# A list scheduler that is told of the tensor engine's divisions

## The chip, the cores and the metric

The kernel runs on one core of a Trainium2 chip. The metric is device microseconds of one execution; lower is better. Three runs of the kernel before took 1682.05, 1683.13 and 1686.35 us, median 1683.13 us.

The core has a tensor engine (PE; its weight loads are shown as an engine of their own, PEld), a vector engine (DVE), a scalar engine (ACT), GpSimd (POOL) and a queue that issues DMAs (SP). Each of them takes its instructions strictly in the order in which they were written; semaphores hold an instruction back until what it needs is there.

## The reference

One layer of a hybrid encoder trunk on 512 tokens of width 1024, in float32:

```
h = rmsnorm(x, norm_mix)
y_a = rwkv7_mixer(h @ wi[:, :OFF_HGRN], ...)        # 16 heads of 64
y_b = hgrn2_mixer(h @ wi[:, OFF_HGRN:OFF_SSM], ...) # 8 heads of 128
y_c = mamba2_mixer(h @ wi[:, OFF_SSM:OFF_GATE], ...) # 4 groups of 8 heads of 64
gates = sigmoid(h @ wi[:, OFF_GATE:]).reshape(b, s, 3, D_MODEL)
merged = gates[:, :, 0] * (y_a @ wb[:1024]) + gates[:, :, 1] * (y_b @ wb[1024:2048])
       + gates[:, :, 2] * (y_c @ wb[2048:])
x = x + merged @ w_out
gate, up = split(rmsnorm(x, norm_ffn) @ w_ffn_in, 2)
x = x + (silu(gate) * up) @ w_ffn_out
out = rmsnorm(x, norm_final)
```

The RWKV mixer is a recurrence over tokens that is computed in chunks of 64; HGRN2 needs decayed scores within chunks, built from small blocks; Mamba-2 is computed in chunks of 128.

## The kernel before, in words

The three mixers share the tensor engine. Dense projections split every float32 operand in a high and a low part (tiles `hh` and `hl`, `wh` and `wl`) and run three passes of 128 x 512 for each pair of 128 x 128 weights (`mm3`, `dense_h`, `dense_cm`). Those, the transposes against `ident` and most other matmuls use all 128 rows and 128 columns of the array. Three kinds of work use a part of it:

- the RWKV chain (`quads`, called from `r_stage1` and `r_chain`): 64 rows by 64 columns, one quarter of the array for each of two heads;
- the HGRN score blocks (`blocks` in `hgrn`): 128 rows by 32 columns, four strips side by side; 16 matmuls make a group, with a PSUM tile `m` (so named in the profile, as `m<-X` or `m<-q,k`);
- a few with 128 rows by 64 columns (the first HGRN level, a narrow projection), 64 rows by 128 columns (two transposes in `r_inverse`) and 32 rows.

I call such a pair of row and column counts a division of the array.

Nothing is written in the order of the source. The class `Recorder` takes down every operation with what it depends on, and `flush` then writes the instructions of all engines by list scheduling: it runs a clock of its own for each engine with estimated durations (`cost`, `passes`, `xfer`), takes the engine that is free first, and gives it, of the operations that are ready by then, the one of the lowest priority number. RWKV's chain has 0, its first stage 1, HGRN 2, Mamba-2 3, the 24 gate projections 4 (PSUM tile `g`, weights `gwh` and `gwl`), the first three parts of the merge 5, and the rest 6. So gates serve as filler wherever nothing more urgent is ready, and everything from the last part of the merge on comes after the mixers. ACT has an exception already: work with the table that is loaded may go ahead of work that needs another table.

For the tensor engine `flush` keeps, for each of the 4 x 4 cells of 32 rows by 32 columns, when its weights were loaded and when its last pass ends (`self.pe`); `passes` tells it how long an operation loads weights, how long each pass streams, and which cells it uses. It lets a load run under the pass before it, whatever the divisions of the two.

Of the kernel before, what the change touches and what calls it, by code (L numbers as in the profile page):

```python
# [74 lines left out]
class Queue:  # L75


    def __init__(self, rec, name):
        self.rec, self.name = rec, name
# [5 lines left out]
class Recorder:  # L85
# [6 lines left out]
    def __init__(self, tc):  # L92
        self.tc, self.nc = tc, tc.nc
        for e in self.ENGINES:
            if e != "gate":
                setattr(self, e, Queue(self, e))
        self.ops, self.done = [], 0
        self.prio = 0
        self.writes, self.reads, self.acc = {}, {}, {}
        self.gate, self.tiles_dram = {}, set()  # L100
        self.tiles, self.proto, self.views = [], {}, set()
        self.tags, self.prev, self.before, self.dead = {}, {}, {}, set()
        self.free = dict.fromkeys(self.ENGINES, 0.0)
        self.table = None
        self.dma = 0.0

        self.pe, self.pe_last = [[(0.0, 0.0)] * 4 for _ in range(4)], 0.0
        self.parts = {}
        self.port = {"vector": 0.0, "gpsimd": 0.0}

# [91 lines left out]
    def passes(self, out, method, args):  # L202


        n = 1
        for d in out.shape[1:]:
            n *= d
        load = args[1].shape[-1] / 1200
        if method == "transpose" or args[1].dtype == F32R:
            ps = [n / (1200 if method == "transpose" else 2226)]  # L210
        else:
            ps = [n / 1200] * 2
        rows, cols = ((q[1] // 32, -(-q[2] // 32)) for q in (self.region(args[1]), self.region(out)))
        return load, ps, [(i, j) for i in range(*rows) for j in range(*cols)]

    def shares(self, eng, method, args, kw, out):

# [84 lines left out]
    def flush(self):  # L302
        ops, lo, n = self.ops, self.done, len(self.ops)
        succ = [[] for _ in range(n - lo)]
        need = [0] * (n - lo)
        ready = [0.0] * (n - lo)
        fut = {e: [] for e in self.ENGINES}
        now = {e: [] for e in self.ENGINES}

        def lat(j, eng):  # L310
            e = ops[j][0]
            if e == eng:
                return {"vector": 0.13, "sync": 2.0, "tensor": -0.3}.get(e, 0.0)
            if e == "sync":
                return 1.0 if ops[j][9] > 0.5 else 2.05
            if e == "gate":
                return 0.0
            if eng == "tensor":
                return 0.17 if e == "scalar" else 0.15
            return 0.21 if e == "tensor" else 0.14  # L320

        def push(k):
            heapq.heappush(fut[ops[lo + k][0]], (ready[k], k))

        for k in range(n - lo):
            op = ops[lo + k]
            for j in op[5]:
                if j >= lo:
                    succ[j - lo].append(k)
                    need[k] += 1  # L330
                else:
                    ready[k] = max(ready[k], ops[j][8] + lat(j, op[0]))
            if not need[k]:
                push(k)
        order, left = [], n - lo
        while left > len(order):
            best = None
            for e in self.ENGINES:
                if now[e]:
                    t = self.free[e]  # L340
                elif fut[e]:
                    t = max(self.free[e], fut[e][0][0])
                else:
                    continue
                if best is None or t < best[0]:
                    best = (t, e)
            t, e = best
            while fut[e] and fut[e][0][0] <= t:
                k = heapq.heappop(fut[e])[1]
                heapq.heappush(now[e], (ops[lo + k][6], k))  # L350
            k = now[e][0][1]
            if e == "scalar" and self.switch(ops[lo + k]) and ops[lo + k][6] and t - ready[k] < 3:
                c = [x for x in now[e] if not self.switch(ops[lo + x[1]])]
                if c:
                    k = min(c)[1]
            now[e].remove((ops[lo + k][6], k))
            heapq.heapify(now[e])
            op = ops[lo + k]
            if e == "scalar" and self.switch(op):
                t += 1.28  # L360
                self.table = op[7]
                order.append(-1 - lo - k)
                left += 1
            if e == "tensor":
                load, ps, parts = op[9]
                loaded = max([ready[k]] + [self.pe[i][j][0] for i, j in parts])
                end = max(self.pe[i][j][1] for i, j in parts)
                for d in ps:
                    loaded = self.pe_last = max(loaded + load, end + 0.003, self.pe_last + 0.006)
                    end = loaded + d  # L370
                for i, j in parts:
                    self.pe[i][j] = (loaded, end)
                op[4] = end - t
            t = max(t, ready[k])
            if e in ("vector", "scalar"):

                if self.parts.get(e) not in (None, op[11]) and t - self.free[e] < 0.1:
                    t = max(t, self.free[e] + 0.11)
                self.parts[e] = op[11]
            if e != "gate" and op[10]:  # L380
                t = max(t, self.port["gpsimd" if e == "vector" else "vector"])
                self.port[e] = t + op[4]
            op[8] = t = t + op[4]
            if e != "gate":
                self.free[e] = op[8]
                order.append(lo + k)
                if e == "sync":
                    op[8] = self.dma = max(op[8] + 0.65, self.dma) + op[9]
            else:
                left -= 1  # L390
            for m in succ[k]:
                ready[m] = max(ready[m], op[8] + lat(lo + k, ops[lo + m][0]))
                need[m] -= 1
                if not need[m]:
                    push(m)
        with self.tc.manual_schedule():
            for j in order:
                if j < 0:
                    self.nc.scalar.preload_act_table_set(ops[-1 - j][7])  # L399
                    continue  # L400
                eng, method, args, kw = ops[j][:4]
                getattr(getattr(self.nc, eng), method)(*[self.resolve(x) for x in args],  # L402
                                                       **{k: self.resolve(x) for k, x in kw.items()})
                ops[j][2:4] = (None, None)
        self.done = n
# [1232 lines left out]
```

## Time and profile before

| | before |
|---|---|
| median of 3 runs | 1683.13 us |
| the profiled execution | 1686.82 us, its span 1685.0 us |
| PE busy | 1630.3 us (97%) |
| PEld busy | 1321.4 us (78%) |
| DVE busy | 1031.7 us (61%) |
| ACT busy | 835.6 us (50%) |
| POOL busy | 267.1 us (16%) |
| granted PE clock, mean | 0.993 |

The span runs from the first instruction to the last; the execution's own time has 1.8 us around it. All recorded operations have one source line in the profile (L402, the line where `flush` issues them; L411 in the changed kernel), so work is told apart by its tiles. In a row such as `PE L402 MATMUL rw<-Ot,SB 64*64 64x64 f32` the part `64*64` is the division, rows by columns. A plain float32 matmul stands in the trace as two passes with a weight load each, a transpose or a pass over split operands as one.

### The profile page before, as it was taken

To read this page: it belongs to the slowest core of one execution; us is meant where nothing else is said; L and a number is where in the kernel's file an instruction comes from. 1 tells how busy PE (TensorE), PEld (TensorE's weight loads), DVE (VectorE), ACT (ScalarE), POOL (GpSimd) and SP (SyncE) were. 2 spreads that over 40 slices of the span, in tenths; PEclk is the share of its full clock that TensorE was granted. 3 is DMA by queue.
4 is the path that set the end of the run, shared out by engine and by line. 5 is a ranking of instruction groups with operands and counts; after the bars stand their busy time and mean duration, and the time that the engine had idled before them with its cause. 6 is when DMAs were issued, how large, how long until landed. Compare 5 with 4: busy or idle time off the path is not lost.

```text
span 1685.0 us, 32049 instructions
## 1 busy us (share of the span) xinstructions
PE 1630.3 (97%) x12302; PEld 1321.4 (78%) x12302; DVE 1031.7 (61%) x2327; ACT 835.6 (50%) x1523; POOL 267.1 (16%) x285
## 2 busy tenths in 40 slices
PE   6999999999999999999999999999999999999998
PEld 5787788777777787788898787777788888888886
DVE  5788888878687878757648748344453533333233
ACT  6666654555466547556647855333433533333222
POOL 1123221313122222003014204011020000000000
PEclk9999999999999999999999999999999999999999
DMA  5334323233233333334424545777572333333232
GB/s 160 85 85 101 90 61 97 77 95 92 65 90 93 86 80 97 90 91 116 122 76 138 154 135 162 241 232 226 175 219 76 113 94 94 94 94 94 95 99 76
DMA packets 291321, 192.09 MB, mean 114 GB/s; under 512 B 59053, under 2 KB 255047, under 8 KB 291167
## 3 DMA queue, kind: packets, MB, share of 16 engines
q1 hardware_dynamic: 291167, 190.04, 39.7%
q8 instruction: 97, 1.59, 0.4%
q14 instruction: 57, 0.47, 0.1%
HBM read 164.22 MB, written 25.76 MB: 113 GB/s over the span
## 4 chain that ended last, share of the span: by engine, by line
PE 81%; DMA 6%; ACT 4%; DVE 4%; issue 2%; SPq 1%; POOL 1%; POOLq 0%; ACTq 0%; DVEq 0%
PE d L402 23%; PE rd L402 17%; PE g L402 10%; PE rw L402 8%; PE rs L402 8%; PE m L402 8%; PE ru L402 7%; SPq L402 1%; ACT L399 1%; DMA wr<-in_w_in_dram 1%; DMA em<-ydram 1%; DMA a<-in_rwkv_a_up_dram 1%; DMA ab<-ydram 1%; DMA cb<-dcum 1%; DVE wl L402 1%
## 5 line engine op out<-in xcount | busy, mean ns | idle before, releaser
L402 DVE TENSOR_TENSOR wl<-wr,wh 128x512 fp32r<-128x512 f32 x267 | 188.4, 707 | 247.4 <-ACT wh L402 239.3
L402 ACT CAST wh<-wr 128x512 fp32r<-128x512 f32 x267 | 164.8, 619 | 342.2 <-PE d L402 119.9
L402 ACT CAST rgh<-rgr 128x512 fp32r<-128x512 f32 x142 | 87.9, 619 | 189.6 <-PE rd L402 89.6
L402 DVE TENSOR_TENSOR rgl<-rgr,rgh 128x512 fp32r<-128x512 f32 x142 | 100.7, 710 | 118.0 <-ACT rgh L402 116.3
L402 PE MATMUL d<-hh,wh 128*128 128x512 f32 (+1 forms) x368 | 147.8, 402 | 7.4 <-DVE q L402 3.5
L402 PE MATMUL d<-hh,wl 128*128 128x512 f32 (+1 forms) x368 | 144.7, 393 | 1.1 <-DVE wl L402 1.1
L402 PE MATMUL d<-hl,wh 128*128 128x512 f32 (+1 forms) x368 | 145.1, 394 | 0.0
L399 ACT ACT_TABLE_LOAD x105 | 134.7, 1283 | 1.8
L402 PE MATMUL rd<-hh,rgh 128*128 128x512 f32 (+1 forms) x324 | 129.6, 400 | 1.0 <-DVE k L402 0.5
L402 PE MATMUL rd<-hl,rgh 128*128 128x512 f32 (+1 forms) x324 | 128.9, 398 | 0.0
L402 PE MATMUL rd<-hh,rgl 128*128 128x512 f32 (+1 forms) x324 | 128.2, 396 | 0.0
L402 PEld LDWEIGHTS d<-hh,wh 128*128 128x128 f32 x368 | 69.5, 189 | 24.9 <-issue 4.4
L402 PE MATMUL g<-hh,gwh 128*128 128x512 f32 x192 | 80.3, 418 | 6.7 <-ACT gwh L402 4.2
L402 PEld LDWEIGHTS d<-hh,wl 128*128 128x128 f32 x368 | 69.4, 189 | 15.2 <-DVE wl L402 1.4
L402 POOL TENSOR_TENSOR X<-X,q 128x256 f32<-128x256 f32 x56 | 51.6, 930 | 181.7 <-ACT X L402 143.9
L402 PEld LDWEIGHTS d<-hl,wh 128*128 128x128 f32 x368 | 69.6, 189 | 12.7 <-issue 0.6
L402 PE MATMUL g<-hh,gwl 128*128 128x512 f32 x192 | 78.1, 407 | 0.2
L402 PE MATMUL g<-hl,gwh 128*128 128x512 f32 x192 | 77.9, 406 | 0.0
L402 PE MATMUL d<-wh,hh 128*128 128x256 f32 x256 | 73.5, 287 | 1.3 <-ACT v L402 0.8
L402 PEld LDWEIGHTS rd<-hh,rgh 128*128 128x128 f32 x324 | 61.3, 189 | 16.7 <-DVE k L402 1.6
L402 PE MATMUL d<-wl,hh 128*128 128x256 f32 x256 | 73.3, 286 | 0.0
L402 PE MATMUL d<-wh,hl 128*128 128x256 f32 x256 | 72.7, 284 | 0.0
(1509 smaller groups left out, 4294.4 us busy)
## 6 DMA issues: line engine op xcount, KB each, us to landing
wr<-in_w_in_dram SPq DMA_DIRECT2D x108, 256.0 KB
rgr<-in_w_in_dram SPq DMA_DIRECT2D x88, 256.0 KB
wr<-in_w_branch_dram SPq DMA_DIRECT2D x59, 256.0 KB
wr<-in_w_ffn_in_dram SPq DMA_DIRECT2D x58, 256.0 KB
gwr<-in_w_in_dram SPq DMA_DIRECT2D x96, 128.0 KB
rgr<-in_w_ffn_in_dram SPq DMA_DIRECT2D x30, 256.0 KB
wr<-in_w_ffn_out_dram SPq DMA_DIRECT2D x30, 256.0 KB
gdram<-gwr SPq DMA_DIRECT2D x24, 256.0 KB
```

The costliest lines, as they stand in the source:

```text
L399: self.nc.scalar.preload_act_table_set(ops[-1 - j][7])
L402: getattr(getattr(self.nc, eng), method)(*[self.resolve(x) for x in args], **{k: self.resolve(x) for k, x in kw.items()})
```

## The change

`passes` returns the division of an operation besides its cells. `flush` remembers the division of the last tensor operation (`pe_mode`) and does two things with it. If the division changes, the first weight load of the new operation may end no earlier than 0.09 us after the last pass on any of the 16 cells; that is, the estimate has the array drain. And while the division is a partial one, ready work of that same division goes before all other ready work, whatever its priority; within it the lowest number still goes first. When the whole array is in use, the choice is as before.

```
-        self.pe, self.pe_last = [[(0.0, 0.0)] * 4 for _ in range(4)], 0.0
+        self.pe, self.pe_last, self.pe_mode = [[(0.0, 0.0)] * 4 for _ in range(4)], 0.0, None
...
-        return load, ps, [(i, j) for i in range(*rows) for j in range(*cols)]
+        return load, ps, [(i, j) for i in range(*rows) for j in range(*cols)], (rows[1] - rows[0], cols[1] - cols[0])
...
+            if e == "tensor" and self.pe_mode not in (None, (4, 4)):
+                c = [x for x in now[e] if ops[lo + x[1]][9][3] == self.pe_mode]
+                if c:
+                    k = min(c)[1]
...
-                load, ps, parts = op[9]
+                load, ps, parts, mode = op[9]
                 loaded = max([ready[k]] + [self.pe[i][j][0] for i, j in parts])
                 end = max(self.pe[i][j][1] for i, j in parts)
+                if mode != self.pe_mode:
+
+                    loaded = max(loaded, max(x[1] for r in self.pe for x in r) + 0.09 - load)
+                    self.pe_mode = mode
```

All engines' orders shift with it, since the estimates decide what is ready when. The tensor engine issues the same 9526 operations (12302 passes); the first 88 and the last 2183 stand in the same order, and half of all are moved by 31 places or more. ACT gets three more table loads.

The first place is on PE near 295 to 302 us of the trace before. `m_1264`, `m_1266`, `m_1268` and `m_1269` are groups of HGRN blocks, `rw_508` and `rw_624` quarters of the RWKV chain, `rs` transposes and `d_1281` a projection of HGRN. Before:

```order
L402 MATMUL m_1264_3957<-X_1263_3786 32x32 x5
L402 MATMUL m_1266_4067<-X_1265_3881 32x32 x10
L402 MATMUL rd_562_4080<-xa_57_383,lwh_559_3931 128x512
...
L402 MATMUL rs_490_4095<-ident_1_93,v_462_3792 128x128 x4
L402 MATMUL m_1266_4067<-X_1265_3881 32x32 x6
L402 MATMUL d_1281_3784<-hl_3_176,wh_1283_3674 128x512
...
L402 MATMUL m_1269_4121<-q_1227_3137,k_1217_2598 32x32 x4
L402 MATMUL rw_624_4127<-UV_489_4108,KAo_480_4057 64x64 x16
L402 MATMUL rs_492_4151<-ident_1_93,BK_474_3569 128x128 x4
L402 MATMUL m_1269_4121<-q_1227_3137,k_1217_2598 32x32 x12
L402 MATMUL d_1281_3784<-hl_3_176,wh_1283_3674 128x512
```

The same operations now:

```order
L411 MATMUL rs_491_4049<-ident_1_93,AR_473_3497 128x128 x4
L411 MATMUL m_1264_4059<-X_1263_3853 32x32 x16
L411 MATMUL m_1266_4079<-X_1265_3870 32x32 x16
L411 MATMUL rw_624_4099<-UV_489_4032,KAo_480_4003 64x64 x16
L411 MATMUL rs_492_4118<-ident_1_93,BK_474_3547 128x128 x4
L411 MATMUL m_1269_4124<-q_1227_3145,k_1217_2686 32x32 x16
L411 MATMUL d_1281_4147<-hh_2_168,wh_1283_3659 128x512
```

A group of 16 blocks that stood in two pieces with other divisions between them now stands in one piece, and two groups follow each other.

The second place is on PE near 700 us, between two projections, `d_1598` and `d_1606`, that use the one PSUM tile `d` in turn; `g_2313` and `g_2299` are gates. Before:

```order
L402 MATMUL d_1598_9489<-hh_2_168,wl_1604_9107 128x512
L402 MATMUL m_1674_9686<-ident_1_93,k_1588_9484 128x128 x3
L402 MATMUL g_2313_8869<-hl_3_176,gwh_2324_9291 128x512
L402 MATMUL g_2313_8869<-hh_2_168,gwl_2325_9305 128x512
L402 MATMUL d_1606_9714<-hh_2_168,wh_1608_9176 128x512
```

Now, with 26 passes of 128 x 512 and 14 transposes between the two, of which the first and the last few are shown:

```order
L411 MATMUL d_1598_9356<-hh_2_168,wl_1604_9053 128x512
L411 MATMUL g_2299_9594<-hh_2_168,gwh_2301_8850 128x512
L411 MATMUL g_2299_9594<-hl_3_176,gwh_2301_8850 128x512
L411 MATMUL m_1674_9598<-ident_1_93,k_1588_9324 128x128
L411 MATMUL m_1586_9602<-ident_1_93,X_1585_9545 128x128 x4
...
L411 MATMUL g_2299_9594<-hh_2_168,gwl_2308_9626 128x512
L411 MATMUL g_2299_9594<-hh_2_168,gwh_2310_9649 128x512
L411 MATMUL g_2299_9594<-hl_3_176,gwh_2310_9649 128x512
L411 MATMUL g_2299_9594<-hh_2_168,gwl_2311_9653 128x512
L411 MATMUL g_2299_9594<-hh_2_168,gwh_2310_9649 128x512
L411 MATMUL d_1606_9684<-hh_2_168,wh_1608_9099 128x512
```

Gate `g_2299` was used up earlier before, and `g_2313` stood here; now there is more of the gates left at this place.

The third place is on PE near 640 us: `m_1526` reads `cb_1525`, which ACT copies out of the transposes `m_1524`. Before:

```order
L402 MATMUL rd_1896_8481<-hl_3_176,rgh_1901_7865 128x512
L402 MATMUL rd_1896_8481<-hh_2_168,rgl_1902_7886 128x512
L402 MATMUL g_2299_7544<-hh_2_168,gwl_2311_8004 128x512
L402 MATMUL m_1524_8850<-ident_1_93,X_1523_8760 128x128 x3
L402 MATMUL m_1526_8862<-v_1480_8081,cb_1525_8858 128x128 x2
L402 MATMUL m_1526_8862<-v_1481_8474,cb_1525_8858 128x128
```

Now:

```order
L411 MATMUL m_1524_8832<-ident_1_93,X_1523_8727 128x128 x3
L411 MATMUL d_1543_8837<-hh_2_168,wh_1545_8457 128x512
L411 MATMUL d_1543_8837<-hl_3_176,wh_1545_8457 128x512
L411 MATMUL d_1543_8837<-hh_2_168,wl_1546_8464 128x512
L411 MATMUL d_1543_8837<-hh_2_168,wh_1545_8457 128x512
L411 MATMUL d_1543_8837<-hl_3_176,wh_1545_8457 128x512
L411 MATMUL d_1543_8837<-hh_2_168,wl_1546_8464 128x512
L411 MATMUL m_1526_8855<-v_1480_7977,cb_1525_8846 128x128 x2
L411 MATMUL m_1526_8855<-v_1481_8357,cb_1525_8846 128x128
```

Six passes of a projection now stand between the transposes and what reads their copy.

## Rows read from the trace of the kernel before

**Rows 1.** The page: span, engines, granted clock, chain that ended last, table loads.
```profile
span 1685.0 us, 32049 instructions
PE 1630.3 (97%) x12302; PEld 1321.4 (78%) x12302; DVE 1031.7 (61%) x2327; ACT 835.6 (50%) x1523; POOL 267.1 (16%) x285
...
PE 81%; DMA 6%; ACT 4%; DVE 4%; issue 2%; SPq 1%; POOL 1%; POOLq 0%; ACTq 0%; DVEq 0%
...
L399 ACT ACT_TABLE_LOAD x105 | 134.7, 1283 | 1.8
```
**Rows 2.** Stretch and length; busy PE, PEld, DVE, ACT, POOL; PEclk, DMA, GB/s.
```profile
100.00:700.00 600.00, 581.16 (x7026) 462.97 (x7025) 485.89 (x1346) 336.37 (x635) 146.22 (x151) 0.99 0.34 86
700.00:1200.00 500.00, 485.87 (x2601) 399.26 (x2600) 287.56 (x517) 271.56 (x483) 88.73 (x90) 0.99 0.52 154
1200.00:1600.00 400.00, 399.96 (x1807) 326.32 (x1806) 161.15 (x252) 139.97 (x244) 12.60 (x12) 1.00 0.37 112
```
**Rows 3.** Waits of PE: us in total, times, longest.
```profile
PE m L402 <- DMA ident<-in_shape_constants_dram: 7.7, 1, 7.7
PE g L402 <- ACT gwh L402: 4.2, 4, 2.6
PE d L402 <- DVE q L402: 3.5, 2, 3.3
```
**Rows 4.** Timeline of PE at 210 us: start, length, instruction, count.
```profile
209.69 0.50 PE L402 MATMUL d<-hh,wh 128*128 128x512 f32 x1
210.02 0.40 PE L402 MATMUL d<-hl,wh 128*128 128x512 f32 x1
210.35 0.33 PE L402 MATMUL rw<-Ot,SB 64*64 64x64 f32 x2
210.60 0.50 PE L402 MATMUL d<-hh,wl 128*128 128x512 f32 x1
210.94 0.40 PE L402 MATMUL d<-hh,wh 128*128 128x512 f32 x1
```
**Rows 5.** Timeline of PE at 279 us, into a block of 32 columns.
```profile
279.55 0.40 PE L402 MATMUL d<-hh,wl 128*128 128x512 f32 x1
279.87 0.52 PE L402 MATMUL ru<-v,yt 128*32 128x128 f32 x5
```
**Rows 6.** Timeline of PE at 302 us, out of a block of 32 columns.
```profile
302.06 0.40 PE L402 MATMUL m<-q,k 128*32 128x32 f32 x24
302.38 0.50 PE L402 MATMUL d<-hl,wh 128*128 128x512 f32 x1
302.72 0.40 PE L402 MATMUL d<-hh,wl 128*128 128x512 f32 x1
```
**Rows 7.** Timeline of PE at 700 us, where `d` waits (last bracket: idle before, releaser).
```profile
699.65 0.40 PE L402 MATMUL d<-hl,wh 128*128 128x512 f32 x1
699.89 0.39 PE L402 MATMUL d<-hh,wl 128*128 128x512 f32 x1
700.12 0.49 PE L402 MATMUL m<-ident,k 128*128 128x128 f32 x3
...
704.40 0.48 PE L402 MATMUL d<-hh,wh 128*128 128x512 f32 x1 [3.32 <-DVE q L402]
```
**Rows 8.** Timeline of PE at 640 us and at 508 us.
```profile
642.49 0.94 PE L402 MATMUL m<-v,cb 128*128 128x128 f32 x6 [1.68 <-ACT cb L402]
...
509.91 0.50 PE L402 MATMUL d<-hh,wh 128*128 128x512 f32 x1 [1.22 <-ACT q L402]
```
**Rows 9.** PE alone in stretches with many 64 x 64 quarters: length, PE busy, PEclk, DMA.
```profile
291.00:295.80 4.80, 4.51 (x126) 1.00 0.27 45
442.40:445.80 3.40, 2.23 (x69) 1.00 0.62 165
447.10:454.20 7.10, 6.94 (x126) 0.60 0.34 67
```
**Rows 10.** All engines around clock changes: columns as in Rows 2.
```profile
446.00:453.00 7.00, 5.85 (x102) 5.38 (x102) 2.94 (x8) 1.91 (x5) 0.00 (x0) 0.52 0.34 68
705.30:708.70 3.40, 3.40 (x12) 2.82 (x11) 1.50 (x2) 2.01 (x3) 0.00 (x0) 0.50 0.46 161
1073.00:1077.40 4.40, 1.78 (x8) 1.12 (x7) 1.12 (x2) 1.50 (x3) 0.00 (x0) 1.00 1.08 393
1077.40:1080.80 3.40, 3.40 (x10) 2.64 (x9) 0.00 (x0) 1.28 (x2) 0.00 (x0) 0.50 1.00 338
```

## The prediction

> **What bounds the kernel now.** I read the page first: PE is busy for 1630.3 of 1685.0 us, and 81% of the chain that ended last is PE [rows 1]. DVE (61%) and ACT (50%) have room. So a microsecond less on PE is a microsecond off the end, and work elsewhere counts only where PE waits for it. The stages come next [rows 2]: from 1200 to 1600 us PE is never without work (399.96 of 400), while it is idle for 600 - 581.16 = 18.8 us between 100 and 700 and for 500 - 485.87 = 14.1 us between 700 and 1200. The last 2183 operations keep their order, and they begin at about 1191 us, so the change can move those 33 us of waits and the work before them, and nothing later. The list of waits [rows 3] says that they are many: the longest, 7.7 us for the constants, is at the start, where the first 88 operations keep their order; behind it come 4.2 us in four waits for gate weights and 3.5 us in two for a PSUM tile that DVE empties. Last I read the timeline of PE around changes of division.
>
> **What a change of division costs.** Between two passes of 128 x 512 of one division lie 0.24 us from start to start (699.65 to 699.89) [rows 7]. Where quarters follow such a pass it is 0.33 us (210.02 to 210.35) [rows 4], where 32 columns follow it is 0.32 us (279.55 to 279.87) [rows 5]: about 0.10 us in which the array runs empty. The first weight load behind it can't run under the pass before, either: the first full pass behind a block takes 0.34 us to the next (302.38 to 302.72) [rows 6], another 0.10. So a change into full width costs 0.20 us. A load of 64 or 32 columns is shorter; I scale the 0.10 to 0.05 and 0.03, an estimate, so 0.15 and 0.13 us. One round trip bears this out: from 210.02 to 210.94 there are two full passes (0.48) and two quarter passes [rows 4], which leaves 0.44 where I price the two changes at 0.35 and the quarters have the rest.
>
> **Term 1, changes saved.** In the order of the kernel before I count 292 changes, in the new one 268. Into 128 columns they go from 148 to 140, into 64 columns from 77 to 82, into 32 columns from 67 to 46. So HGRN's blocks are gathered (of their 67 pieces 46 are left, as the first place in the order shows), while RWKV's quarters are cut a little more often, because their chain is one of dependences and seldom has more ready. Sum: -8 x 0.20 + 5 x 0.15 - 21 x 0.13 = -3.6 us. Bounds: the empty time alone, 24 x 0.10 = 2.4 us; all at the highest price, 24 x 0.20 = 4.8 us. None of it lies beside other work of PE, so all of it counts.
>
> **Term 2, waits that are covered or made.** The larger effect may be the estimate. The scheduler now believes PE slower by 0.09 us a change, so it thinks that other engines' results come after less work on PE, and reaches for filler less often. In the order, 216 gate passes stood on PE ahead of the last RWKV output; now 180 do. Ahead of the transposes `rs_2008` of Mamba-2's third group it was 294, and is 242. 52 passes x 0.24 = 12 us of filler are kept for later. Three waits of before can be followed into the new order:
> - At 704.40 `d` waits 3.32 us for DVE to empty it; from its last pass at 699.89 that is 4.5 us [rows 7]. Three transposes and two gate passes stood between, now 26 passes of 128 x 512 and 14 transposes: 26 x 0.24 = 6.2 us alone, more than 4.5. The wait is covered, and with it perhaps the clock at half speed behind it: 0.50 over 3.4 us (705.3 to 708.7) [rows 10] loses 1.7 us. Together 5.0 us.
> - At 642.49 the wait for ACT's copy `cb` is 1.68 us [rows 8]; six passes now stand there, 6 x 0.24 = 1.4 us.
> - At 509.91 it is 1.22 us [rows 8]; five gate passes between the two uses of `d` are now six and four small matmuls, for some 0.6 us.
>
> That is 7.0 us. But the order is shuffled as a whole, and a shuffle makes new waits as it removes old ones; these three I found because I looked for the long ones of before. I keep half, -3.5 us. Bounds: all of it, -7.0 us, and a third of the 33 us of waits more or less, 11 us, either way.
>
> **What I price at nothing.** Blocks that go ahead of urgent work delay it: 24 block passes take 0.32 us (302.06 to 302.38) [rows 6], so the longest gathered piece, 36 blocks in 72 passes, holds an RWKV step up for about 1 us. PE works meanwhile, and gates fill in behind; without gates it would be 1 us for each such piece. ACT gets three more table loads, 3 x 1.283 = 3.8 us [rows 1]; it is busy half the time, so they are covered, and cost up to 3.8 us if each stood in front of a copy that PE waits for. DVE, POOL and the DMA queue issue the same operations; a weight load on that queue moves by five places in the median, and none gets a wait that it did not have.
>
> **Sum.** -3.6 - 3.5 = -7.1 us on the profiled execution: 1686.8 - 7.1 = 1679.7. That execution is 3.7 us above the median of the runs, 1683.1, so I forecast 1676 us.
>
> **Rivals.**
> - *More filler helps the second half too.* Between 700 and 1200 us there are 14.1 us of waits [rows 2] and the clock at half speed behind 1077 [rows 10] loses 1.7 us more. With 12 us more of gates left there, half of this might go beyond what I count: 8 us, so 1668. Against it: the filler waits itself, 4.2 us in four waits for gate weights [rows 3].
> - *Only the changes count.* New waits equal the covered ones: 1683.1 - 3.6 = 1679.5, or up to the old time if they are a little more. For it: none of the waits is caused by a division, so nothing in the change aims at them. It also covers that the change hardly does what it says: 24 changes of 292 is 8%.
> - *Slower: longer stretches of quarters bring the clock down.* At 442.4 to 445.8 PE was busy with quarters for 2.23 of 3.4 us, at full clock, and from 446 to 453 the granted clock was 0.52 [rows 9, 10]: 7.0 x 0.48 = 3.4 us lost, and 1.2 us of wait. This is one of RWKV's eight head pairs. The longest stretches of quarters without a change were 112, 72, 72 and 72 operations, and are now 125, 122, 116 and 91. If these four bring a piece each, that is 3 x 4.6 = 13.8 us more; with term 1 and nothing covered, 1683.1 - 3.6 + 13.8 = 1693. From three pieces on it decides against the change. Against it: at 291.0 to 295.8 the same kind of stretch, 126 passes, is busy for 4.51 of 4.80 us and the clock stays at 1.00 [rows 9], and rule and diff only prefer work that is ready, so they add no wait of their own. The Trainium skill (TensorE: Matmul & The Clock Gate, "A second HAM failure mode: psum-queue depth-cycling") says that small idle times between groups of matmuls that cycle through PSUM banks are enough to make the clock swing between its two levels. By that page most of the long stretches would bring a piece; this trace agrees at one pair and not at the others.
> - *Slower: filler meets the transfers.* At 1073 us gates wait while the DMA engines are at 1.08 and 393 GB/s, PE has 1.78 of 4.4 us, and the clock is 0.50 for the 3.4 us after [rows 10]: 2.6 + 1.7 = 4.3 us. More gates are left for this stage now. Three more such waits make 1676 + 13 = 1689.
>
> **How the numbers follow.** The forecast has 0.38, the first rival 0.14, the second 0.29, the clock 0.12, the transfers 0.07. A measurement of this kernel can tell about 0.3%, 5 us. The first rival and nearly all of the forecast's case are faster by more than 5 us (below 1678): 0.50; the second and the edge of the forecast's are within it: 0.31; the last two are slower: 0.19. The likeliest case has 1671 to 1680 of its own. The range, 1664 to 1690, takes in the helpful filler, no change and the slower cases in part, and leaves out some 5% below and 10% above.
>
> **What would show it.** Right: changes of division cost 0.1 us of empty array as before and are 268; the 3.3 us wait of `d` behind DVE and the half clock at 705 are gone; gates stand later; PE's idle time between 100 and 1200 us is below 33 us by a few. Wrong: idle time of PE between 100 and 700 us well above 18.8 us, mostly of quarters behind copies, or more pieces at half clock than before; then the tighter order cost more than the changes gave. If the idle time is the same and the end moved by 3 to 4 us, only term 1 was real.

## The result

The changed kernel took 1697.08 us in the median of four runs (1693.91 to 1699.34), the kernel before 1682.59 us on the same occasion: 1.008 of it, with a 95% interval of 1.0057 to 1.0104. I had forecast 1676 us. It is slower by some 14 us, and outside the range.

The profiled execution took 1698.34 us. The page of the changed kernel, the lines that answer to [rows 1] (its mean granted clock is 0.989):

```profile
span 1696.6 us, 32036 instructions
...
PE 1636.1 (96%) x12302; PEld 1329.3 (78%) x12302; DVE 1028.2 (61%) x2327; ACT 839.6 (49%) x1526; POOL 267.1 (16%) x285
...
PE 80%; DVE 7%; ACT 5%; DMA 3%; issue 3%; SPq 1%; POOL 1%; POOLq 0%; DVEq 0%; ACTq 0%
...
L408 ACT ACT_TABLE_LOAD x108 | 138.6, 1283 | 1.8
```

The span is 11.6 us longer. PE's idle time went from 1685.0 - 1630.3 = 54.7 to 1696.6 - 1636.1 = 60.5 us, which is 5.8 of it; the other 5.8 us are more busy time with the same work. The granted clock tells what that is: its mean fell from 0.993 to 0.989, that is from 0.007 x 1685 = 11.8 to 0.011 x 1697 = 18.7 us lost to half clock, 6.9 us more. So the clock accounts for all of the added busy time: without it PE would have been busy about as long as before, or some 1 us less, which is no more than the rounding of the two means (0.8 us each). The mean clock of the other three executions was 0.991 to 0.992, so this one shows the larger share of half clock.

By stage, in the changed kernel (as [rows 2]: stretch, its length, PE, PEld, DVE, ACT, POOL, PEclk, DMA share, GB/s):

```profile
100.00:700.00 600.00, 578.27 (x7036) 465.82 (x7035) 476.84 (x1332) 342.96 (x638) 149.74 (x152) 0.99 0.34 84
700.00:1200.00 500.00, 486.23 (x2610) 399.47 (x2609) 292.74 (x528) 268.19 (x486) 86.54 (x91) 0.99 0.52 153
1200.00:1600.00 400.00, 400.00 (x1806) 326.20 (x1806) 159.89 (x249) 139.81 (x244) 12.57 (x12) 1.00 0.38 113
```

PE is idle for 21.7 us in the first stretch (18.8 before) and for 13.8 us in the second (14.1). Another 3 us came in the first 100 us (81.8 us busy against 85.0). The clock, PE alone (stretch, length, busy, PEclk, DMA share, GB/s; 0.50 is the lower of the clock's two levels, 1.2 in place of 2.4 GHz):

```profile
90.20:97.00 6.80, 5.55 (x13) 0.50 0.11 33
138.00:141.40 3.40, 2.73 (x61) 1.00 0.58 153
141.40:148.20 6.80, 6.29 (x115) 0.50 0.07 20
230.20:233.60 3.40, 1.50 (x49) 1.00 0.28 45
233.60:237.00 3.40, 3.40 (x26) 0.50 0.21 46
377.00:380.40 3.40, 2.41 (x59) 0.99 0.08 23
380.40:383.80 3.40, 3.40 (x105) 0.51 0.00 0
448.60:452.00 3.40, 2.68 (x69) 1.00 0.58 132
452.00:455.50 3.50, 3.50 (x47) 0.51 0.17 50
731.90:735.30 3.40, 3.40 (x10) 0.50 0.50 147
```

Five pieces at half clock lie between 50 and 700 us, where before there was the one at 446 [rows 10]; behind 700 us there are two (732 and 1097) in place of three (705, 944 and 1077). Ahead of those at 141, 233, 380 and 452 us PE worked 2.73, 1.50, 2.41 and 2.68 of 3.4 us, and waited for DVE, mostly with quarters; ahead of the first stands the longest new wait.

The list of PE's waits, of the changed kernel (us in total, times, longest), against [rows 3]. Its first line is the wait at the start of the kernel, which was 7.7 us before and put down to a DMA; the others are to be compared:

```profile
PE m L411 <- DVE SB L411: 7.5, 1, 7.5
PE ru L411 <- DVE AR L411: 4.8, 6, 0.9
PE g L411 <- ACT gwh L411: 4.7, 5, 1.5
PE rd L411 <- ACT a L411: 3.5, 1, 3.5
PE g L411 <- ACT gwr L411: 3.5, 2, 2.9
```

The wait of 3.3 us of `d` at 704 us is gone, as worked out: `g` and `d` follow each other without a gap. But 20 us later the gate's own PSUM tile is what PE stands at. PE and ACT of the changed kernel (start, length, instruction, in brackets the idle time before it and its releaser):

```profile
709.68 0.40 PE L411 MATMUL g<-hh,gwh 128*128 128x512 f32 x1
709.91 0.47 PE L411 MATMUL d<-hh,wh 128*128 128x512 f32 x1
```
```profile
727.68 0.40 PE L411 MATMUL g<-hh,gwl 128*128 128x512 f32 x1
...
729.06 1.28 ACT L408 ACT_TABLE_LOAD   x1
...
730.35 0.60 ACT L411 ACTIVATE gwr<-g 128x512 f32<-128x512 f32 x1
...
731.00 0.50 PE L411 MATMUL g<-hh,gwh 128*128 128x512 f32 x1 [2.92 <-ACT gwr L411]
```

ACT does two other activations and loads a table before it empties `g`, PE waits 2.92 us, and the clock is 0.50 from 731.9 on. The wait at 88 us has the same form: ACT loads a table from 88.83 to 90.13, does `tmpA`, then `a`, which empties `rd`:

```profile
87.41 0.50 PE L411 MATMUL rd<-xa,lwl 64*128 64x512 f32 x1
...
88.83 1.28 ACT L408 ACT_TABLE_LOAD   x1
90.13 0.69 ACT L411 ACTIVATE tmpA<-rs,par 128x512 f32<-128x512 f32 x1
90.72 0.68 ACT L411 ACTIVATE a<-rd,par 128x512 f32<-128x512 f32 x1
...
91.45 0.79 PE L411 MATMUL rd<-hh,rgh 128*128 128x512 f32 x1 [3.54 <-ACT a L411]
92.04 0.63 PE L411 MATMUL rd<-hl,rgh 128*128 128x512 f32 x1
92.47 0.63 PE L411 MATMUL rd<-hh,rgl 128*128 128x512 f32 x1
```

Behind it a pass starts 0.43 us or more after the other in place of 0.24. In the order before, ACT did the same load and the same two activations, from 90.16 us on, but PE had passes of a projection to run meanwhile, and no wait (PE alone, kernel before):

```profile
85.00:90.20 5.20, 5.20 (x44) 1.00 0.26 60
90.20:97.00 6.80, 6.80 (x58) 1.00 0.27 78
```

Of the other two waits that the prediction followed, the one for `cb` at 640 us is gone (651.86 us here). The use of `d` at 508 us before is at 518.82 us here, and its wait fell from 1.22 to 0.35 us; one of 1.28 us has come up at the projection ahead of it:

```profile
509.84 0.50 PE L411 MATMUL d<-hh,wh 128*128 128x512 f32 x1 [1.28 <-DVE lf L411]
...
518.82 0.50 PE L411 MATMUL d<-hh,wh 128*128 128x512 f32 x1 [0.35 <-DVE cum L411]
...
651.86 0.83 PE L411 MATMUL m<-v,cb 128*128 128x128 f32 x6
```

The price of a change of division is what it was, as [rows 4] and [rows 6]: out of a block of 32 columns 0.34 us to the next pass, into half the rows 0.33 us.

```profile
209.81 0.39 PE L411 MATMUL m<-X 128*32 128x32 f32 x25
210.12 0.50 PE L411 MATMUL d<-hl,wh 128*128 128x512 f32 x1
210.46 0.40 PE L411 MATMUL d<-hh,wl 128*128 128x512 f32 x1
210.79 0.33 PE L411 MATMUL ru<-ident,Yq 64*128 64x64 f32 x2
```

### The profile page after: what moved, and what is told of

It is laid out like the page before. It is cut to its first block, busy times and chain, and to the rows that moved or that the text cites. A ratio compares the mean times of both kernels' runs of the same rounds, so it can differ in the third digit from the quotient of the medians.

```text
span 1696.6 us, 32036 instructions
## 1 busy us (share of the span) xinstructions
PE 1636.1 (96%) x12302; PEld 1329.3 (78%) x12302; DVE 1028.2 (61%) x2327; ACT 839.6 (49%) x1526; POOL 267.1 (16%) x285
## 4 chain that ended last, share of the span: by engine, by line
PE 80%; DVE 7%; ACT 5%; DMA 3%; issue 3%; SPq 1%; POOL 1%; POOLq 0%; DVEq 0%; ACTq 0%
PE d L411 23%; PE rd L411 16%; PE g L411 10%; PE rw L411 8%; PE rs L411 8%; PE ru L411 7%; PE m L411 7%; ACT L408 1%; DVE X L411 1%; ACT ab L411 1%; SPq L411 1%; DMA ab<-ydram 1%; DVE wl L411 1%; DVE SB L411 1%; DVE gwl L411 0%
## 5 line engine op out<-in xcount | busy, mean ns | idle before, releaser
L411 POOL TENSOR_TENSOR X<-X,q 128x256 f32<-128x256 f32 x56 | 56.0, 1009 | 185.2 <-ACT X L411 145.6
L411 PEld LDWEIGHTS rd<-hh,rgh 128*128 128x128 f32 x324 | 61.5, 190 | 22.4 <-ACT a L411 4.5
L411 PEld LDWEIGHTS rd<-hh,rgl 128*128 128x128 f32 x324 | 61.5, 190 | 14.5 <-issue 0.5
```

## The experiments

Three theories. **P**: the preference does the harm, since it runs quarters in one stretch and takes the filler out of the RWKV chain. **E**: the estimate does it, since a PE that is believed slow saves filler and stands at other engines' results. **S**: neither; any new order of this length lands somewhere else, mostly above. The runs were made on several occasions, on which the kernel before took 1682.6 to 1686.8 us in the median, so rows are compared by the last column.

| run | changes of division | us, median | of the kernel before, 95% interval |
|---|---|---|---|
| changed kernel | 268 | 1697.1 | 1.0080 (1.0057 to 1.0104) |
| estimate only | 283 | 1687.9 | 1.0018 (1.0005 to 1.0031) |
| preference only | 296 | 1693.0 | 1.0041 (1.0025 to 1.0056) |
| estimate, preference for strips | 244 | 1693.7 | 1.0052 (1.0031 to 1.0072) |
| estimate, preference for quarters | 310 | 1708.1 | 1.0127 (1.0110 to 1.0144) |
| drain at its measured size | 258 | 1698.6 | 1.0081 (1.0058 to 1.0104) |
| change from the 701st operation on | 278 | 1687.0 | 1.0018 (1.0005 to 1.0031) |
| shuffle 1 (table load 1.30) | 286 | 1704.5 | 1.0115 (1.0099 to 1.0132) |
| shuffle 2 (rate 2232) | 291 | 1682.0 | 0.9973 (0.9955 to 0.9991) |
| shuffle 3 (latency) | 284 | 1694.1 | 1.0048 (1.0030 to 1.0066) |
| shuffle 4 (table load 1.26) | 295 | 1684.3 | 0.9985 (0.9973 to 0.9996) |
| shuffle 5 (rate 2236) | 289 | 1686.7 | 0.9998 (0.9988 to 1.0008) |
| change on shuffle 1 | 270 | 1685.5 | 0.9998 (0.9984 to 1.0011) |
| change on shuffle 2 | 255 | 1683.3 | 0.9979 (0.9968 to 0.9990) |
| change on shuffle 4 | 265 | 1689.2 | 1.0036 (1.0024 to 1.0048) |
| change on shuffle 5 | 261 | 1690.7 | 1.0045 (1.0027 to 1.0063) |
| before, gathered on PE alone | 254 | 1683.8 | 0.9995 (0.9984 to 1.0006) |
| shuffle 2, gathered on PE alone | 259 | 1678.9 | 0.9963 (0.9951 to 0.9976) |

**Estimate alone**, the preference never taken:

```
-            if e == "tensor" and self.pe_mode not in (None, (4, 4)):
+            if e == "tensor" and self.pe_mode == "none":
```

> The changed kernel without its preference: the scheduler still believes that a change of division costs 0.09 us of empty array, but always takes the ready work of the lowest number. Its order has 283 changes of division. Theory P (the preference does the harm: quarters of the RWKV chain go in one stretch, and the chain's serial steps lose the filler that stood between): near the time before, 1680 to 1686 us, with one or two pieces at half clock between 50 and 700 us. Theory E (the estimate does it: PE is believed slow, filler is saved, and PE stands at DVE's and ACT's results): near the changed kernel, 1692 to 1699 us, with four or more pieces. Theory S (neither; any new order of this length comes out some 5 to 15 us worse than the one that happened to be good): 1688 to 1697 us.

It is 0.18% slower, 3 us: near the time before, as P expects, or at the lower edge of S, and against E. Its trace has three pieces at half clock between 50 and 700 us (91, 361 and 682), which is between P and E.

**Preference alone**, without the drain:

```
-                    loaded = max(loaded, max(x[1] for r in self.pe for x in r) + 0.09 - load)
```

> The kernel before with the preference alone: ready work of the present partial division goes first, but the scheduler's clock knows of no drain. Its order has 296 changes of division; half of the operations move by 14 places or more. Theory P: slow, 1692 to 1699 us, pieces at half clock behind long stretches of quarters. Theory E: near the time before, 1680 to 1686 us. Theory S: 1688 to 1697 us.

0.41% slower; in the reach of P and S. Its longest piece at half clock, 13.7 us from 209 us on, stands behind a gate that waited 2.06 us for ACT, not behind a stretch of quarters as P has it. Estimate and preference together do more (0.80%) than one and the other (0.59%), but the intervals leave room for a plain sum.

**Strips alone** (`== (4, 1)`) and **quarters alone** (`== (2, 2)`) in the preference's condition, the estimate kept:

> The changed kernel, its preference kept for blocks of 32 columns alone (HGRN's), not for RWKV's quarters; the estimate is kept. 244 changes of division, the fewest of all: 48 fewer than before, which is 7 us by the prices of the prediction. Theory P: 1676 to 1682 us, since quarters are not drawn together by a rule. Theory E: 1690 to 1698 us, as the estimate is in it. Theory S: 1685 to 1697 us.

> The changed kernel with its preference for RWKV's quarters alone, the counterpart of the run with HGRN's strips alone (1693.7 us) and of the estimate alone (1687.9 us). 310 changes of division, 18 more than before. If estimate, strips and quarters add up, from the changed kernel's 1697.1 us: 1697.1 - (1693.7 - 1687.9) = 1691 us. Theory P: most of the harm is here, 1694 to 1699 us. Theory S: they don't add up, anywhere from 1687 to 1698 us.

Strips alone save 48 changes and are 0.52% slower, which P did not allow; E and S did. Quarters alone are 1.27% slower, more than strips and quarters together and more than any of the theories had. So the parts don't add up to the whole, and the fewest changes do not make the fastest kernel.

**The drain at its measured size**:

```
-                    loaded = max(loaded, max(x[1] for r in self.pe for x in r) + 0.09 - load)
+                    loaded = max(loaded, max(x[1] for r in self.pe for x in r) + 0.095)
```

> The changed kernel with the drain at its measured size: the first load starts 0.095 us after the last pass and does not run under it, so that a change costs 0.12 to 0.20 us instead of 0.09 in the scheduler's clock. 258 changes of division, and still less filler early: 168 gate passes ahead of the last RWKV output (216 before, 180 in the changed kernel). Theory E: slower still than the changed kernel, 1698 to 1705 us, with more waits for DVE and ACT between 50 and 700 us. Theory P: as the changed kernel, 1693 to 1699 us. If a truer estimate makes a better order, against both: 1680 to 1690 us.

As slow as the changed kernel, at the meeting point of E and P: a truer figure did not mend the order. In its trace the loss lies elsewhere again: PE is busy for 86.0 us of the first 100 (81.8 in the changed kernel) and for 571.6 of the next 600 (578.3).

**Shuffles without the change**: one constant of the scheduler's estimates moved by 2% or less (3% for the latency).

```
-                t += 1.28
+                t += 1.30
```

> The kernel before with nothing new: one constant of the scheduler's estimates, the ACT table load, at 1.30 us in place of 1.28. It shuffles the order about as much as the change does (half of PE's operations move by 24 places or more; 286 changes of division; 197 gate passes ahead of the last RWKV output, 216 before). Theory S (any shuffle of the order is worse by 5 to 15 us, and the change is mostly one): 1688 to 1697 us. Theories P and E (preference and estimate do harm by what they do): 1680 to 1688 us.

> A second shuffle of the kernel before: the estimated rate of a split pass at 2232 columns per us in place of 2226. Half of the operations move by 36 places or more, 291 changes of division, 191 gate passes ahead of the last RWKV output, as few as in the changed kernel's order. Theory S: 1688 to 1697 us. Theories P and E: 1680 to 1688 us; if it is slow nevertheless, the shuffles' own spread is as large as the effect.

> A third, lighter shuffle: what PE waits behind another engine's result at 0.175 and 0.155 us in place of 0.17 and 0.15. Half of the operations move by 11 places or more, 284 changes of division, 222 gate passes ahead of the last RWKV output. Theory S: 1686 to 1695 us. Theories P and E: 1680 to 1688 us.

They went from 0.27% faster to 1.15% slower. The first is worse than the changed kernel, beyond even what S had, with nothing in it that knows of divisions, and it shows the changed kernel's signs. PE alone in its trace, then its waits:

```profile
202.40:205.90 3.50, 1.21 (x96) 1.00 0.85 202
205.90:219.70 13.80, 12.93 (x70) 0.51 0.21 55
386.90:393.70 6.80, 6.80 (x92) 0.50 0.01 2
```
```profile
PE g L402 <- ACT gwr L402: 9.5, 4, 2.7
...
PE ru L402 <- ACT UV L402: 4.6, 4, 2.1
```

Gates that wait for ACT to empty their PSUM tile, quarters that wait, and 13.8 us at half clock: neither the waits nor the clock need the preference. Nor does the clock need quarters: ahead of the 13.8 us PE ran blocks of HGRN that waited for DVE, and then a gate waited 1.97 us for ACT. The second shuffle, which ran fewer gates early just as the changed kernel does (191 passes ahead of the last RWKV output), is faster than the kernel before; so saved filler alone isn't the harm either.

**The change from the 701st PE operation on.**

```
+                self.npe += 1
-                if mode != self.pe_mode:
+                if mode != self.pe_mode and self.npe > 700:
```

(and the same condition at the preference).

> The changed kernel, its rule and its estimate used from the 701st PE operation on, some 95 us into the span; before that the order is that of the kernel before. In the changed kernel the first 105 us lost 6.0 us: a wait of 3.5 us of PE for ACT behind a table load, and a piece at half clock. If losses are places that add up: 1697.1 - 6.0 = 1691 us. If a different start shuffles everything behind it: anywhere from 1681 to 1708 us, with losses at other places than the changed kernel's (141, 233, 380 and 452 us).

1687.0 us: by the ratios some 10 us less than the changed kernel, with an interval of about 6 to 15, where the first 105 us had cost 6.0. So the time alone does not exclude losses that add up. The trace shows that they did not stay in place: its pieces at half clock between 50 and 1200 us lie at 320, 511, 798 and 1071 us, none at a place of the changed kernel's. Everything behind the first 95 us was drawn anew.

**The change on other shuffles, and two fresh shuffles.** The fresh shuffles (4 and 5) are the kernel before with one constant moved; "the change on" a shuffle is the changed kernel with the one constant of that shuffle.

> The change on the first shuffle (table load estimated at 1.30 us), which without it took 1704.5 us. 270 changes of division there against 286. If the change itself costs 14 us: 1718 us. If it is one shuffle among others: it has no memory of its base, and lies between 1682 and 1705 us, so more likely below 1704.5.

> The change on the second shuffle (stream rate 2232), which without it took 1682.0 us. 255 changes of division against 291. If the change itself costs 14 us: 1696 us. If the saved changes show and nothing else: 1677 us. If it is one shuffle among others: between 1682 and 1705 us.

> A fourth shuffle without the change: the table load estimated at 1.26 us. Half of the operations move by 28 places or more, 295 changes of division, 196 gate passes ahead of the last RWKV output. If the kernel before is an order that happened to be good: 1688 to 1700 us. If shuffles lie around it: 1678 to 1692 us.

> A fifth shuffle without the change: stream rate 2236. Half of the operations move by 33 places or more, 289 changes of division, 192 gate passes ahead of the last RWKV output. If the kernel before is an order that happened to be good: 1688 to 1700 us. If shuffles lie around it: 1678 to 1692 us.

> The change on the fourth shuffle (table load at 1.26 us), which without it took 0.9985 of the kernel before. 265 changes of division against 295. If the change itself costs 14 us: 1.007 of the kernel before. If it is one order among others: 0.997 to 1.011, and no rule tells where.

> The change on the fifth shuffle (rate 2236), which without it took 0.9998 of the kernel before. 261 changes of division against 289. If the change itself costs 14 us: 1.008 of the kernel before. If it is one order among others: 0.997 to 1.011.

In five pairs the change moved the time by +0.80, -1.17, +0.06, +0.51 and +0.47% of the kernel before. The mean is +0.13%, and by the spread of the five its 95% interval reaches from about -0.8 to +1.1%; without the first pair, the one that was to be explained, the mean is -0.03%. Where the scheduler takes a table load at 1.28 us the edit costs 0.80%, where it takes it at 1.30 us the same edit gains 1.17%. If an order has no memory of its base, the two groups can be compared without pairs as well: the kernel before and its five shuffles lie 0.20% above the kernel before in the mean, the five with the change 0.28%. S as I had put it falls in one point: shuffles do not lie above the kernel before, they lie around it.

One loss of the change is no draw. The wait at 88 us, of 3.5 to 3.8 us, stands there (its end between 89 and 92 us) in seven of the nine kernels whose scheduler has the drain in its clock from the start, with half clock behind it in all seven, and in none of the ten others. The estimate alone, then the change on shuffle 1:

```profile
89.80 0.50 PE L411 MATMUL rd<-hh,rgh 128*128 128x512 f32 x1 [3.52 <-ACT a L411]
```
```profile
90.61 0.50 PE L411 MATMUL rd<-hh,rgh 128*128 128x512 f32 x1 [3.55 <-ACT a L411]
```

So the estimate does there what E says, it saves filler that PE then lacks. But it does not decide where an order ends: with this wait the change on shuffles 1 and 2 is as fast as the kernel before or faster, and without it the change on shuffle 5 and the drain at its measured size are slower.

**Gathering without a shuffle.** After the scheduler has ordered everything as in the kernel before, a run of a partial division between two runs of one other division is moved down to the next run that holds the same PSUM tiles, where nothing between needs it. The other engines keep their orders to the last instruction.

```
+        order = self.gather(order, lo, succ)
...
+                for r2 in range(r + 1, min(r + 8, len(runs))):
+                    a2, z2, d2 = runs[r2]
+                    if d2 == d and mine <= {name(order[pe[n]]) for n in range(a2, z2)}:
+                        break
...
+                rest = [j for j in span if j not in moved]
+                order[pe[a]:pe[a2]] = rest + moved
```

> The kernel before, its order left as it is on DVE, ACT, GpSimd and the DMA queue; on PE alone, a piece of a partial division is moved down to the next piece of the same PSUM tile, where nothing between needs it (321 of 9526 places differ). 254 changes of division in place of 292: 11 fewer into full width, 19 fewer into 64 columns, 8 fewer into 32 columns, which by the prediction's prices is 2.2 + 2.9 + 1.0 = 6.1 us. If changes are worth that once nothing else is shuffled: 1679 us, 0.36% under the kernel before. If drains are hidden in waits anyway: no change, 1684 to 1687 us. If longer stretches of quarters bring the clock down: slower, 1688 to 1693 us, with pieces at half clock behind them.

> The same gathering on PE, done to the order of the second shuffle (stream rate; 1682.0 us). 259 changes of division in place of 291: 9 fewer into full width, 14 into 64 columns, 9 into 32, by the prices 1.8 + 2.1 + 1.2 = 5.1 us. If changes are worth their price: 1677 us, under both kernels. If not: 1680 to 1684 us.

This is the measured worth of a change of division. 38 fewer, priced at 6.1 us, gave 0.05% of 1685 us: 0.8 us, between a gain of 2.7 and a loss of 1.0. The full price is excluded. PE of the gathered kernel, by its page (mean granted clock 0.993, as before) and by stage, tells where the rest went:

```profile
PE 1626.5 (97%) x12302; PEld 1322.1 (79%) x12302; DVE 1031.3 (61%) x2327; ACT 835.8 (50%) x1523; POOL 268.1 (16%) x285
...
100.00:700.00 600.00, 577.55 (x7014) 0.99 0.34 86
```

PE is busy for 3.8 us less than before [rows 1], for the same passes at the same clock, so a good part of the price does leave its busy time. But it is idle for 22.4 us from 100 to 700, 3.6 more than in the kernel before [rows 2]: it comes to the same results earlier and waits for them. That is one execution of each. The profiled executions of all 19 kernels say the same more loosely: PE's busy time with the half clock taken off grows by 0.13 us with each change of division (correlation 0.71), but the span hardly goes with their number (0.31). On shuffle 2 the gathering gave 1682.0 to 1678.9 us in the medians, which is between the two expectations, and 0.10% in the ratios, whose intervals overlap. That version is faster than both kernels: 0.9963 of the kernel before (0.9951 to 0.9976).

## Why the prediction was wrong

- **What bounds the kernel**: PE is, on 80% of the chain; nothing moved behind 1200 us, and all of the 11.6 us lie ahead of it. What did not hold is "a microsecond less on PE is a microsecond off the end", as the gathered order shows. And the waits that could be lost or made were put between 100 and 1200 us only, where they rose by 2.5 us; another 3.2 us came ahead of 100 us, at a place where PE had not waited at all.
- **The price of a change of division**: held as a row, 0.33 and 0.34 us against 0.23 in the changed kernel's trace. **Term 1**, its sum, was mis-sized: not each change saved comes off the end. "None of it lies beside other work of PE, so all of it counts" is the sentence that failed. Where the next thing on PE waits for DVE or ACT, an earlier PE only waits longer; the gathered order kept some 0.8 of 6.1 us. In the changed kernel itself the busy time without the half clock fell by about 1 us where 3.6 were forecast.
- **Term 2** is the step that cost the forecast: put at -3.5 us, it measured some +12 us, 5.8 of idle time and 6 to 7 of half clock. Its three followed waits went as worked out: `d` at 704 us and `cb` at 640 us no longer wait long, and the one at 508 us fell by 0.9 us. But they were replaced by waits of 3.54 us at 88 and 2.92 us at 727.7 us and by short ones of quarters. The prediction had said why, that a scheduler which believes PE slow "reaches for filler less often", and followed it only to the places where it helps. I wrote that "a shuffle makes new waits as it removes old ones" and still kept half of the gain, though only the long waits of before had been looked for; the value that this supports is zero, with wide bounds. Its bound of 11 us either way was also too tight, as it left out that new waits bring pieces at half clock.
- **Three table loads more, at nothing**: not settled. Two of the new waits stand behind a table load on ACT, but shuffle 1, the slowest of the shuffles, has three fewer than the kernel before (102 against 105), the change from the 701st operation on seven more, and the fastest order of all five more.
- **The clock rival** saw what the trace would show: half clock behind stretches of quarters, and a price of 1693 us. I gave it 0.12 and put it down to the longer stretches that the preference makes. The page of the Trainium skill cited there says of another kernel, in bf16, that short idle times among matmuls which cycle PSUM banks let the clock swing (TensorE: Matmul & The Clock Gate, "A second HAM failure mode: psum-queue depth-cycling"). The trace agrees ahead of 141, 380 and 452 us: there waits were under 1 us each, PE was busy for 2.73, 2.41 and 2.68 of 3.40 us, and the clock fell. It does not everywhere: from 296.0 to 299.4 us quarters waited twice for DVE, PE was busy for 2.53 of 3.40 us, and the clock stayed at 1.00 there and in the 3.4 us behind. As to the cause the runs don't bear me out: shuffle 1 has more of it without any preference, and with the change on shuffle 1 the mean granted clock is 0.995 where it was 0.988.
- **The other rivals** did not come. Between 700 and 1200 us PE's idle time is the same (13.8 against 14.1 us), so the gates left there helped nothing; and gates wait for their weights 4.7 us in five waits where it was 4.2 in four, so they did not meet the transfers more than before.
- **The range**: five shuffles without the change spread from -0.27 to +1.15%, some 24 us. The range had that width, 26 us, but was laid around the forecast's gain of 7 us: from 19 us under the time before to 7 above, where shuffles go from 5 under to 19 above. It should have been laid around no change at the least.

What stays open: whether the drain estimate or the preference has a worth or cost of its own at the end of some tenths of a per cent; five pairs can't show it, though the wait at 88 us is the estimate's own. Why some short waits bring the clock down and others do not, the runs do not tell. And why shuffles 1 and 2 are 22 us apart is located (waits of PE at DVE and ACT, and the clock behind them), not traced to one cause.

## What to carry to other kernels

An edit to a list scheduler is two things: its rule, and a new draw of the whole order. Measure the draw first, by moving a constant that should not matter, and compare the rule over several draws; and where the rule can be had as a local edit to a finished order, measure it so. A stall saved on the busiest engine is worth only what the next wait behind it does not take back, and an order's waits are paid twice where the clock comes down behind them. Filler that a scheduler saves has to be missed somewhere: look for the places that had no wait because of it.

## What the runs showed of the hardware that I had not expected

The clock can cost as much as the waits. Between the profiled executions of shuffle 2 gathered, the fastest order, and of shuffle 1, the slowest of the shuffles (spans 1672.6 and 1697.2 us), the mean granted clock went from 0.997 to 0.988: 5.0 against 20.4 us lost at half clock, which is 15 of the 25 us between them. PE of the former, by its page:

```profile
PE 1622.6 (97%) x12302; PEld 1319.8 (79%) x12302; DVE 1032.8 (62%) x2327; ACT 843.0 (50%) x1528; POOL 267.7 (16%) x285
```

Its busy time is 13.5 us below the changed kernel's for the same 12302 passes. That execution is the fastest of its order's eight, whose clocks went down to 0.991, so the share is not the order's alone. In the slowest kernel of all, quarters alone, the clock matters less: of the 21.7 us that its span is above that of the kernel before, 10.0 are idle time of PE and some 4 half clock (mean 0.991).

One and the same order has such a spread, too. In 101 executions of the kernel before the time went from 1679.0 us, at a mean clock of 0.997, to 1690.5 us, at 0.990 (correlation of time and clock over all of them -0.80). Seven thousandths of 1685 us are 11.8 us, as much as the two are apart: from one execution to the next it is mostly the clock that differs.
